# Sums of the adaLN columns turned in 32 by 32 blocks on VectorE, with the order of all instructions set anew, in a two-layer attention trunk

## The chip, the cores and the metric

The kernel runs on one core of a Trainium2 chip. The metric is the device time of one execution in microseconds. Engines are named as in the profile: PE (TensorE's matmuls) and PEld (its weight loads), DVE (VectorE), ACT (ScalarE), POOL (GpSimd), SP (SyncE, which issues nearly all transfers).

## What is computed

The input x has 256 rows of 1,024 in fp32, and c is one row of 1,024. Two layers follow each other; cut to what matters here:

```
c_act = silu(c)
for layer in range(2):
    ada = c_act @ w_ada[layer] + b_ada[layer]          # 1024 -> 3072
    shift, scale, gate = split(ada, 3)
    h = rms_norm(x, norm_g[layer]) * (1 + scale) + shift
    y = even_mixer(h, ...) if layer == 0 else odd_mixer(h, ...)
    x = x + gate * y
return rms_norm(x, final_g)
```

The even mixer is one input projection (2,840 columns), two groups of attention heads (a sliding window with sinks; a sparse one with a compressed, a selected and a window branch), a gate, and an output projection. The odd mixer projects to 4,096 columns, attends in blocks, gates and projects back.

## The kernel before, in words

**Layout.** Activations lie with features on the 128 partitions. `hhi` and `hlo` hold the normed input of a layer in two parts, `ghi` and `glo` the gated attention's output; each weight is split the same way, on ACT (`whi`, a cast) and on DVE (`wlo`, the rest), and every product is three matmuls, hi by hi, hi by lo and lo by hi (`mm3`). The weights come in through a ring of five buffers, `raw` (`raw_106` to `raw_110` in the rows below); `whi` and `wlo` have four buffers each. PSUM's banks are shared out as ps_pj (3), ps_s (2), ps_pt, ps_o and ps_m.

**The order.** No engine's code is in the order in which the work is written down. Each call is recorded as an operation with what it depends on (`Plan.record`, lines 242 to 277), and at the end `Plan.issue` emits all of them in the order of a table of some 3,000 numbers, `ORDER` (line 35 on), which thereby sets the order on each engine and on each queue. A second table, `FLIP`, lists the copies, scalings and affine steps that go to the other of ACT and DVE. In the profile all operations have the line of the recorded call, L276, so they are told apart by their tiles. `record` also keeps ACT's functions of different tables apart: an operation of one kind depends on all those of the other kind before it (line 273).

**The columns of shift and scale, layer 0.** `cz` holds silu(c) in column 0 of 32 columns for each of the 8 row blocks, zeros elsewhere, and a one at [:, KT, 0]. The features are done in groups of n = 1, 2, 2, 2 and 1 blocks of 128 (`START`, line 24). For a group `start_ada` (line 719 on) loads the columns of `w_ada` into whatever room is free (the tiles `qT`, `gate`, `oT`, `kTb`, `t`), and `start_sums` (line 731) forms the sums over the rows: the first d row blocks on DVE into `acc`, the others on PE, as fp32 matmuls with `cz` as weights in four tiles of 32 columns of the array side by side. So the sums of 128 columns come out along a row in one of four partitions (0, 32, 64 and 96) of the bank `ps_m`, with zeros in the other partitions. With n = 2 each of the four holds one block of shift or scale, all row blocks summed; with n = 1 two of them share a block, even row blocks in one and odd ones in the other. The rows are turned to columns: copied to `asb` (128x128, on ACT or DVE), turned by PE with `ident` (n = 2) or multiplied with the two columns of `blk` (n = 1), back into `ps_m`; DVE adds the biases from there into `shs`. Then `start_prep` makes `hhi` and `hlo` of these features by an affine step, and `start_mm` adds their products to the eight accumulators of the first projection.

**Layer 1's columns.** While layer 0 runs, DVE sums the rows of `w_ada[1]` into the fifth buffer of the ring (`raw_110`) by `ada_sums`, 16 passes of 1,024 columns, as loads come in between those for the weights. `ada_shift_scale` (line 476) then takes this sum over the partitions by four matmuls of 512 columns with `cz`, ACT copies them to a `t` tile, PE turns it in four pieces with `ident`, and DVE adds the biases from `ps_m` into `shs`. At the hand-over from layer 0 to layer 1 (lines 1132 to 1150) the row tile t is scaled by the reciprocal root of its mean square (each half on DVE or ACT), turned on PE, and `hhi` and `hlo` are made by affine steps with `shs`; the first product of layer 1 takes `hhi` as its right side.

Of the kernel before, what the change touches and what calls it, by code (L numbers as in the profile page):

```python
# [287 lines left out]
def tile_trunk(  # L288
# [187 lines left out]
    def ada_shift_scale(l, accs):  # L476
# [3 lines left out]
        for q in range(4):  # L480
            ids.append(T.matmul(pa[32 * q : 32 * q + 32, :], cz[:, KT, :], accs[q], start=True, stop=True, tile_position=(0, 32 * q)))
# [919 lines left out]
```

## Time and profile before

| what | value |
|---|---|
| median of 3 runs | 294.73 us (293.92 to 294.83) |
| the profiled execution's own time | 295.43 us |
| its span (first to last instruction) | 293.7 us |
| granted clock of TensorE | 0.996 |
| busy share: PE, PEld, DVE, ACT, POOL | 97%, 83%, 86%, 69%, 2% |
| read from memory | 70.32 MB |

The profile has one execution's instructions with start, duration, tile, shape and the operation whose end released a wait ("idle before, releaser"). The time lies 1.7 us over the span. A matmul of fp32 operands shows as two records, so a count of x16 is eight matmuls. The chain of work that ended last follows what released each instruction back from the end of the span.

### The profile page before, as it was taken

How to read it: one execution, taken by the hardware profiler on the slowest of the kernel's cores; microseconds unless marked ns; L12 is line 12 of the kernel's file. 1: busy time of each engine (PE TensorE's matmuls, PEld its weight loads, DVE VectorE, ACT ScalarE, POOL GpSimd, SP SyncE). 2: the span in 40 equal slices, each digit the busy share in tenths (PEclk: the TensorE clock that was granted, in tenths of full speed). 3: DMA queues.
4: the chain of work that ended last, by engine and by line, in shares of the span. 5: the costliest groups of instructions: out<-in, count | busy, mean ns of one | idle time of the engine just before them, and what ended most of it. 6: DMA issues, size and time to landing. Idle time of an engine off the chain costs nothing.

```text
span 293.7 us, 6077 instructions
## 1 busy us (share of the span) xinstructions
PE 283.5 (97%) x2244; PEld 243.5 (83%) x2244; DVE 253.0 (86%) x612; ACT 201.2 (69%) x513; POOL 5.5 (2%) x27
## 2 busy tenths in 40 slices
PE   8989999999999999999899999999999999999991
PEld 7868888997789888777667799999799899887891
DVE  0669999999999999999899868898699889889973
ACT  5554746695999999996398744466667377783821
POOL 2100000000000000000000000000000000000000
PEclk9999999999999999999999999999999999999998
DMA  7999999987996787799996449608927661604003
GB/s 260 364 385 377 383 355 353 311 287 237 342 400 212 264 281 293 213 323 361 305 372 216 146 143 329 243 4 296 351 71 249 237 234 34 227 27 145 1 15 129
DMA packets 50557, 71.76 MB, mean 244 GB/s; under 512 B 2792, under 2 KB 36192, under 8 KB 50528
## 3 DMA queue, kind: packets, MB, share of 16 engines
q1 hardware_dynamic: 50128, 70.95, 70.7%
q10 hardware_dynamic: 400, 0.43, 0.4%
q8 instruction: 17, 0.28, 0.4%
q14 instruction: 12, 0.10, 0.1%
HBM read 70.32 MB, written 1.06 MB: 243 GB/s over the span
## 4 chain that ended last, share of the span: by engine, by line
PE 73%; DVE 13%; DMA 8%; issue 2%; ACT 2%; SPq 0%; DVEq 0%
PE ps_pj L276 49%; PE ps_s L276 9%; PE ps_pt L276 6%; DVE raw L276 5%; PE ps_o L276 4%; PE ps_m L276 4%; DMA kTb<-in_w_ada_dram 3%; DMA raw<-in_w_ada_dram 2%; DVE wlo L276 2%; DMA qT<-in_w_ada_dram 2%; DMA xs<-in_x_dram 1%; DVE t L276 1%; DVE oT L276 1%; ACT t L276 1%; DVE bigA L276 1%
## 5 line engine op out<-in xcount | busy, mean ns | idle before, releaser
L276 ACT CAST whi<-raw 128x512 fp32r<-128x512 f32 (+2 forms) x108 | 71.6, 689 | 33.6 <-PE ps_pj L276 15.8
L276 DVE TENSOR_TENSOR wlo<-raw,whi 128x512 fp32r<-128x512 f32 (+2 forms) x92 | 70.8, 792 | 6.4 <-ACT whi L276 6.4
L276 PE MATMUL ps_pj<-hlo,whi 128*128 128x256 f32 x256 | 70.8, 284 | 0.0
L276 PE MATMUL ps_pj<-hhi,wlo 128*128 128x256 f32 x256 | 70.0, 284 | 0.3 <-DVE wlo L276 0.3
L276 PE MATMUL ps_pj<-hhi,whi 128*128 128x256 f32 x256 | 69.9, 284 | 0.0
L276 PEld LDWEIGHTS ps_pj<-hlo,whi 128*128 128x128 f32 x256 | 48.0, 189 | 0.6 <-issue 0.3
L276 PEld LDWEIGHTS ps_pj<-hhi,wlo 128*128 128x128 f32 x256 | 47.4, 189 | 0.7 <-DVE wlo L276 0.5
L276 PEld LDWEIGHTS ps_pj<-hhi,whi 128*128 128x128 f32 x256 | 47.4, 188 | 0.3
L276 ACT ACTIVATE sm<-sm,mn 128x256 f32<-128x256 f32 (+1 forms) x58 | 25.9, 449 | 6.9 <-DVE mn L276 6.9
L276 PE MATMUL ps_pj<-whi,hhi 128*128 128x512 f32 (+2 forms) x72 | 25.8, 368 | 0.5 <-ACT hhi L276 0.4
L276 PE MATMUL ps_pj<-whi,hlo 128*128 128x512 f32 (+2 forms) x72 | 26.1, 374 | 0.0
L276 PE MATMUL ps_pj<-wlo,hhi 128*128 128x512 f32 (+2 forms) x72 | 26.0, 370 | 0.0
L276 DVE SCALAR_TENSOR_TENSOR wlo<-raw,whi 128x512 fp32r<-128x512 f32 x32 | 20.6, 686 | 3.7 <-ACT whi L276 3.6
L276 PE MATMUL ps_pj<-wlo,ghi 128*128 128x512 f32 (+1 forms) x56 | 20.4, 368 | 0.0
L276 PE MATMUL ps_pj<-whi,ghi 128*128 128x512 f32 (+1 forms) x56 | 20.4, 369 | 0.0
L276 PE MATMUL ps_pj<-whi,glo 128*128 128x512 f32 (+1 forms) x56 | 20.0, 367 | 0.0
L276 ACT ACTIVATE sm<-sm,rc 128x256 f32<-128x256 f32 (+1 forms) x41 | 17.3, 449 | 2.3 <-DVE rc L276 2.3
L276 DVE SCALAR_TENSOR_TENSOR raw<-raw,cz,raw 128x1024 f32<-128x1024 f32 x14 | 17.9, 1276 | 1.0 <-DMA raw<-in_w_ada_dram 0.9
L276 DVE SCALAR_TENSOR_TENSOR acc<-raw,cz,acc 128x1024 f32<-128x1024 f32 x14 | 17.9, 1278 | 0.1
L276 PEld LDWEIGHTS ps_pj<-whi,hhi 128*128 128x128 f32 x72 | 13.6, 188 | 2.7 <-ACT hhi L276 1.2
L276 PEld LDWEIGHTS ps_pj<-whi,hlo 128*128 128x128 f32 x72 | 13.5, 188 | 2.5 <-DVE hlo L276 0.8
L276 PE MATMUL ps_pt<-ident,sm 128*128 128x128 f32 x87 | 15.5, 279 | 0.0
(252 smaller groups left out, 599.7 us busy)
## 6 DMA issues: line engine op xcount, KB each, us to landing
raw<-in_w_in_odd_dram SPq DMA_DIRECT2D x16, 1024.0 KB, 7.5
raw<-in_w_ada_dram SPq DMA_DIRECT2D x8, 1024.0 KB, 6.2
raw<-in_w_ada_dram SPq DMA_DIRECT2D x16, 512.0 KB, 5.2
raw<-in_w_in_even_dram SPq DMA_DIRECT2D x8, 652.0 KB, 7.2
raw<-in_w_in_even_dram SPq DMA_DIRECT2D x5, 1024.0 KB, 7.7
raw<-in_w_out_even_dram SPq DMA_DIRECT2D x4, 1024.0 KB, 5.4
raw<-in_w_out_odd_dram SPq DMA_DIRECT2D x4, 1024.0 KB, 5.0
qT<-in_w_ada_dram SPq DMA_DIRECT2D x12, 256.0 KB, 6.2
```

What stands on the lines that cost most here:

```text
L276: self.ops.append(dict(key=eng.key, deps=deps, fn=lambda: getattr(real, name)(*args, **kw)))
```

## The change

**The turning.** Instead of a copy, a turn on PE and adds from PSUM, DVE turns the sums straight from PSUM into SBUF in blocks of 32 by 32 (`V.transpose`, STREAM_TRANSPOSE in the rows), and the adds read SBUF. For that the four tiles of 32 array columns no longer hold a block each: tile q now takes columns 32q to 32q + 31 of every 128-column block (the strided `cq` and `aq`), so that a turn by 32 by 32 blocks puts each sum on its own partition. A group of n blocks turns 64n columns, layer 1's turns 512. With n = 1 each tile now sums all row blocks, in 64 columns instead of 128: the first group's sums are 32 matmuls of 64 columns (64 records) in place of 16 of 128, the last group's 20 (40 records) in place of 10.

**The tables.** An operation of a table kind now also depends on the first one of its own kind (`self.since[:1]`), so that the small activation that brings a table's load goes ahead of the others. `ORDER` and `FLIP` are new throughout.

```diff
-            deps |= set(self.before)
+            deps |= set(self.before + self.since[:1])
...
-            ids.append(T.matmul(pa[32 * q : 32 * q + 32, :], cz[:, KT, :], accs[q], start=True, stop=True, tile_position=(0, 32 * q)))
+            aq = accs.rearrange("p (b e) -> p b e", e=P)[:, :, 32 * q : 32 * q + 32]
+            ids.append(T.matmul(pa[32 * q : 32 * q + 32, :], cz[:, KT, :], aq, start=True, stop=True, tile_position=(0, 32 * q)))
         plan.group(ids)
         asb = t4()[:, :512]
-        copy(A, asb, pa)
-        pc = bank("m")
-        for o in range(0, 512, P):
-            T.transpose(pc[:, o : o + P], asb[:, o : o + P], ident)
-        pv = pc.rearrange("p (c h s e) -> p h s c e", c=4, h=2, s=2)[:, :, :, :, 0]
+        V.transpose(asb, pa)
+        pv = asb.rearrange("p (h s c e) -> p h s c e", h=2, s=2, e=32)[:, :, :, :, 0]
...
-            s_, j, ks = (q // 2, 0, range(q % 2, KT, 2)) if n == 1 else (q // 2, q % 2, range(KT))
-            cs = slice(j * P, (j + 1) * P)
-            tq = [(cz[:, k, :], w[k][:, s_, cs]) for k in ks if k >= d]
-            if d and 0 in ks:
-                tq.append((cz[:, KT, :], av[:, s_, cs]))
-            terms.append(tq)
+            cq = lambda v: v.rearrange("p s (j e) -> p (s j) e", e=P)[:, :, 32 * q : 32 * q + 32]
+            terms.append([(cz[:, k, :], cq(w[k])) for k in range(d, KT)] + ([(cz[:, KT, :], cq(av))] if d else []))
...
-        asb = sb([P, 2 * P], "asb", 2)
-        copy(A, asb[:, :P], pa[:, :P])
-        pc = bank("m")
+        asb = sb([P, 2 * P], "asb", 2)[:, : 64 * n]
+        V.transpose(asb, pa[:, : 64 * n])
...
-        if n == 1:
-            T.matmul(pc[:, 0:2], asb[:, :P], blk[:, 6:8], start=True, stop=True)
...
-            T.transpose(pc[:, :P], asb[:, :P], ident)
...
+        pv = asb.rearrange("p (s j e) -> p s j e", s=2, e=32)[:, :, :, 0]
+        V.tensor_tensor(shs[:, 0, :, gs], pv, bs, ALU.add)
+        V.tensor_tensor(shs[:, 0, 1, gs], shs[:, 0, 1, gs], ngT[:, gs], ALU.mult)
```

In all PE has 1,902 instructions in place of 1,885, DVE 619 in place of 615, ACT 430 in place of 434. Three transpositions of `asb`, four of `t`, two products with `blk`, and six copies of sums (two on DVE, four on ACT) go; six turns on DVE come. Of the copies and scalings that `FLIP` moves, three 128x384 copies (`kTb`) and two 128x512 ones (`bigA`) go from DVE to ACT, and three 128x128 scalings (`sm`) the other way, among others. In the start SP issues, behind x, both pieces of `qT0`, then the 384 columns of the first projection rows, a piece of `qT1`, and only then the 1,304 columns that stood second; the two pieces of `kTb` stood together behind `gate`, and now the first goes out between `gate`'s two pieces and the second still behind all of that group.

PE, in the start, around the second group's sums (`kTb` and `acc` with `cz`, into `ps_m_68`), among the products of the first projection. Before:

```order
L276 MATMUL ps_pj_101<-wlo_116,hhi 128x512
L276 MATMUL ps_pj_100<-wlo_116,hhi 128x512
L276 MATMUL ps_s_97<-wlo_116,hhi 128x512
L276 MATMUL ps_m_68<-kTb,cz 32x128 x8
L276 MATMUL ps_m_68<-acc_111,cz 32x128 x4
L276 MATMUL ps_s_98<-whi_112,hhi 128x512
L276 MATMUL ps_s_97<-whi_112,hlo 128x512
L276 MATMUL ps_m_68<-ident,asb_86 128x128
```

After:

```order
L275 MATMUL ps_s_98<-whi_112,hhi 128x512
L275 MATMUL ps_s_98<-wlo_116,hhi 128x512
L275 MATMUL ps_pt_90<-wlo_117,hhi 128x256
L275 MATMUL ps_m_68<-oT,cz 32x128 x8
L275 MATMUL ps_m_68<-kTb,cz 32x128 x8
L275 MATMUL ps_m_68<-acc_111,cz 32x128 x4
L275 MATMUL ps_s_97<-wlo_116,hhi 128x512
L275 MATMUL ps_o_70<-wlo_117,hhi 128x408
```

The group's first sums, `oT` with `cz`, which stood 17 rows ahead of `kTb`'s before, now stand next to them, and the transposition with `ident` four rows further on is gone.

PE, the last group's sums of the start (the same tiles, n = 1). Before:

```order
L276 MATMUL ps_o_70<-whi_113,hhi 128x408
L276 MATMUL ps_m_68<-kTb,cz 32x128 x8
L276 MATMUL ps_m_68<-acc_111,cz 32x128 x2
L276 MATMUL ps_pj_100<-whi_114,hlo 128x512
L276 MATMUL ps_pj_100<-whi_112,hhi 128x512
L276 MATMUL ps_m_68<-blk,asb_85 128x2
```

After:

```order
L275 MATMUL ps_pt_90<-wlo_119,hhi 128x256
L275 MATMUL ps_m_68<-kTb,cz 32x64 x16
L275 MATMUL ps_m_68<-acc_111,cz 32x64 x4
L275 MATMUL ps_pj_100<-whi_112,hhi 128x512
L275 MATMUL ps_pj_99<-whi_115,hlo 128x408
```

Ten matmuls of 128 columns became 20 of 64, and the product with `blk` went.

DVE, the end of layer 0, from the sum that frees `raw_109` to the last piece of layer 1's sums, which is loaded into the same buffer (`oT` and `glo` are the gated outputs, `sm` and `rc` the softmax's). Before:

```order
L276 SCALAR_TENSOR_TENSOR raw_110<-raw_109,cz,raw_110 128x1024
L276 TENSOR_SCALAR sm_126<-sm_126,rc_143 128x256
L276 TENSOR_SCALAR sm_126<-sm_126,rc_143 128x128
L276 SCALAR_TENSOR_TENSOR oT<-ps_o_70,oT 128x256
L276 TENSOR_TENSOR wlo_119<-raw_107,whi_115 128x1024
L276 SCALAR_TENSOR_TENSOR raw_110<-raw_106,cz,raw_110 128x1024 x2
L276 SCALAR_TENSOR_TENSOR oT<-ps_o_70,oT 128x256
L276 TENSOR_TENSOR wlo_116<-raw_108,whi_112 128x1024
L276 TENSOR_TENSOR glo<-oT,ghi 128x512
L276 SCALAR_TENSOR_TENSOR raw_110<-raw_109,cz,raw_110 128x1024 x2
```

After:

```order
L275 SCALAR_TENSOR_TENSOR raw_110<-raw_109,cz,raw_110 128x1024
L275 TENSOR_TENSOR wlo_118<-raw_107,whi_114 128x1024
L275 SCALAR_TENSOR_TENSOR oT<-ps_o_70,oT 128x256
L275 SCALAR_TENSOR_TENSOR raw_110<-raw_106,cz,raw_110 128x1024
L275 TENSOR_TENSOR wlo_119<-raw_107,whi_115 128x1024
L275 SCALAR_TENSOR_TENSOR raw_110<-raw_106,cz,raw_110 128x1024
L275 SCALAR_TENSOR_TENSOR oT<-ps_o_70,oT 128x256
L275 TENSOR_TENSOR wlo_116<-raw_108,whi_112 128x1024
L275 TENSOR_TENSOR glo<-oT,ghi 128x512
L275 SCALAR_TENSOR_TENSOR raw_110<-raw_109,cz,raw_110 128x1024 x2
```

The two products with `rc_143` are out of this stretch, and `wlo_118` is in it.

DVE, the hand-over, from the reciprocal root of the first row tile (`parts`) to the product of the second one's last piece with the gate (`t_96`); `rT` holds the biases and `raw_106`, `raw_107` layer 1's first weights. Before:

```order
L276 RECIPROCAL parts<-parts 128x1
L276 TENSOR_SCALAR rT<-rT 128x8
L276 TENSOR_SCALAR t_94<-xs,parts 128x512
L276 TENSOR_TENSOR shs<-ps_m_68,rT 128x2x4 x2
L276 TENSOR_TENSOR shs<-shs,rT 128x8
L276 TENSOR_TENSOR wlo_118<-raw_106,whi_114 128x512
L276 TENSOR_TENSOR wlo_116<-raw_107,whi_112 128x512
L276 TENSOR_TENSOR t_96<-ps_s_98,gate 128x512
```

After:

```order
L275 RECIPROCAL parts<-parts 128x1
L275 STREAM_TRANSPOSE t_93<-ps_m_68 128x512
L275 TENSOR_TENSOR wlo_119<-raw_106,whi_115 128x512
L275 TENSOR_TENSOR shs<-t_93,rT 128x2x4 x2
L275 TENSOR_TENSOR shs<-shs,rT 128x8
L275 TENSOR_TENSOR wlo_119<-raw_106,whi_115 128x512
L275 TENSOR_TENSOR wlo_116<-raw_107,whi_112 128x512
L275 TENSOR_TENSOR t_96<-ps_s_98,gate 128x512
```

The scaling of `xs` by `parts` left DVE (ACT has both halves now), the turn of `ps_m_68` came in, and one `wlo` stands ahead of `shs`.

More of the change, by code (lines that the diff above doesn't have):

```diff
@@ L511, in shift_scale_jobs @@
         r = [lambda u=u, h=h: ada_sums(l, [(512 * h, 512 * h + 512), (D + 512 * h, D + 512 * h + 512)], 2 * u, 2, raws[4][:, D * h : D * h + D]) for h in range(2) for u in range(4)]
-        return r + [lambda: ada_shift_scale(l, acs)]
+        return r + [lambda: ada_shift_scale(l, raws[4])]
     dp = ctx.enter_context(tc.tile_pool(name="dp", bufs=1, space=bass.MemoryType.DRAM))
@@ L753, in start_sums @@
                     ids.append(T.matmul(
-                        pa[32 * q : 32 * q + 32, :P],
+                        pa[32 * q : 32 * q + 32, : 64 * n],
                         tq[m][0],
@@ L762, in start_sums @@
             plan.group(ids[o : o + 8])
-        asb = sb([P, 2 * P], "asb", 2)
-        copy(A, asb[:, :P], pa[:, :P])
-        pc = bank("m")
+        asb = sb([P, 2 * P], "asb", 2)[:, : 64 * n]
+        V.transpose(asb, pa[:, : 64 * n])
         gs = slice(g, g + n)
         bs = bT[:, 0:16].rearrange("p (s j) -> p s j", s=2)[:, :, gs]
-        if n == 1:
-            T.matmul(pc[:, 0:2], asb[:, :P], blk[:, 6:8], start=True, stop=True)
-            V.scalar_tensor_tensor(shs[:, 0, 1, gs], pc[:, 1:2], bs[:, 1, :], ngT[:, gs], op0=ALU.add, op1=ALU.mult)
-            V.tensor_tensor(shs[:, 0, 0, gs], pc[:, 0:1], bs[:, 0, :], ALU.add)
-        else:
-            T.transpose(pc[:, :P], asb[:, :P], ident)
-            pv = pc[:, :P].rearrange("p (s j e) -> p s j e", s=2, e=32)[:, :, :, 0]
-            V.tensor_tensor(shs[:, 0, :, gs], pv, bs, ALU.add)
-            V.tensor_tensor(shs[:, 0, 1, gs], shs[:, 0, 1, gs], ngT[:, gs], ALU.mult)
+        pv = asb.rearrange("p (s j e) -> p s j e", s=2, e=32)[:, :, :, 0]
+        V.tensor_tensor(shs[:, 0, :, gs], pv, bs, ALU.add)
+        V.tensor_tensor(shs[:, 0, 1, gs], shs[:, 0, 1, gs], ngT[:, gs], ALU.mult)
     def start_row(g):
@@ L1084, in tile_trunk @@
     raws = ring["raw"][0]
-    acs = [raws[4][:, 512 * q : 512 * q + 512] for q in range(4)]
     ring["raw"] = [raws[:4], 0]
```

259 rows, old and new, of tables (FLIP, ORDER) are left out of this document.

## The prediction

> **What bounds the kernel now.** I read the per-core line first, then the busy time by stretches, then the chain of work that ended last, then the timeline around its waits. The one core is granted its full clock, so no term below is a change of clock:
>
> ```profile
> core 0: 293.7 us, clock 0.996
> ```
>
> The stretches (length, busy time of each engine with instruction counts, clock, share of the DMA engines, GB/s):
>
> ```profile
> core 0: us, PE busy (x) PEld busy (x) DVE busy (x) ACT busy (x) POOL busy (x), PEclk, DMA share, GB/s
> 20.00:60.00 40.00, 40.00 (x273) 34.54 (x273) 37.58 (x82) 25.18 (x62) 0.00 (x0) 1.00 1.03 352
> 60.00:103.00 43.00, 43.00 (x415) 36.47 (x415) 42.39 (x149) 38.71 (x124) 0.38 (x3) 1.00 0.85 291
> 103.00:146.00 43.00, 42.63 (x306) 33.01 (x302) 41.94 (x87) 36.28 (x96) 0.32 (x1) 1.00 0.86 296
> ```
>
> PE is without a gap from 20 to 103 us, and DVE is nearly so: it idles 2.42 us in 20 to 60, 0.61 in 60 to 103, 1.06 in 103 to 146. The transfers are full until 60 us. So layer 0 is bound by PE with DVE a hair behind, and there is hardly room for either to take on work. The chain (start, length, what) shows where the end is set by something else:
>
> ```profile
> 11.01 7.55 DMA kTb<-in_w_ada_dram
> ...
> 134.45 6.87 DMA raw<-in_w_ada_dram
> 141.42 1.29 DVE raw L276
> ...
> 145.22 1.14 DVE wlo L276
> ...
> 152.34 0.82 ACT t L276 x2
> ```
>
> Three places, then: a transfer at 11 to 18.6 us, DVE (held once by a transfer) until 146, and the hand-over to layer 1 at 151 to 153.6. After that the chain is PE almost to the end, and the change leaves that stretch and the tail as they were. The first and the last two places are where a moved order can act; 20 to 103 us is where removed PE work counts.
>
> **The change part by part.** *A, the start.* PE's one long stop and the work behind it:
>
> ```profile
> 18.61 0.64 PE L276 MATMUL ps_m<-kTb,cz 128*32 128x128 f32 x16 [1.12 <-DMA kTb<-in_w_ada_dram]
> 20.05 0.62 ACT L276 CAST whi<-raw 128x512 fp32r<-128x512 f32 x1 [2.64 <-DMA raw<-in_w_in_even_dram]
> ```
>
> PE waits 1.12 us for the last piece of kTb, and 1.4 us later ACT waits for the next rows of the projection weights. The new queue order puts the same bytes ahead of both, so both should land when they did, and PE can't come out of the start earlier than those landings let it. What goes is the copy and the transposition between kTb's sums and the next factors (20.0 us), of which one short DVE instruction is left: I take -0.2. If kTb lands sooner, as one of its two pieces now goes out earlier, up to half of the stop goes (-0.6); if the rows that were moved back come late, +0.5.
>
> *B, the PE work that goes from the PE-bound stretch.*
>
> ```profile
> 19.98 0.28 PE L276 MATMUL ps_m<-ident,asb 128*128 128x128 f32 x1
> 48.61 0.28 PE L276 MATMUL ps_m<-blk,asb 128*128 128x2 f32 x2
> 150.74 0.60 PE L276 MATMUL ps_m<-ident,t 128*128 128x128 f32 x4
> ```
>
> Four transpositions take 0.60 and one 0.28, so each further one costs PE (0.60 - 0.28) / 3 = 0.11 us, the rest being the pipeline's depth. Two of them lie after 20 us (the third is in A), and the pair with blk at 48.6 costs something between 0.11 and 0.28, say 0.18: 2 x 0.11 + 0.18 = 0.4. With PE unbroken from 20 to 103 us this comes off the chain: -0.4 (bounds -0.2, if DVE holds PE at once, and -0.5).
>
> *C, the sums of the single blocks in 64 columns.* The last group is issued as 40 records of 64 columns where 20 of 128 stood (each fp32 product shows as two records); the first as 64 where 32 stood, but that one is ahead of PE's 1.12 us stop and costs nothing as long as the stop is there. Prices:
>
> ```profile
> 11.09 0.81 PEld L276 LDWEIGHTS ps_m<-qT,cz 128*32 128x32 f32 x32
> 11.10 1.08 PE L276 MATMUL ps_m<-qT,cz 128*32 128x128 f32 x32
> 47.26 0.66 PE L276 MATMUL ps_m<-kTb,cz 128*32 128x128 f32 x16
> ```
>
> A further record costs (1.08 - 0.66) / 16 = 0.026 us, and the weight load of a record 0.81 / 32 = 0.025. If the columns set the pace, 40 records of 64 cost what 20 of 128 did: 0. If the loads do, which are no shorter for fewer columns, 20 more records cost 20 x 0.025 = +0.5. The two prices are so alike that I believe the loads, and take +0.4. The Trainium skill speaks against the change here: "TensorE: Matmul & The Clock Gate", the section "Wait — 56ns, not 53.3ns?", says that matmuls never start less than about 25 ns apart, however few columns they have; by that this term would be +0.5 (an estimate from the page), and the trace's 0.026 us for 128 columns in four tiles side by side already lies at that floor. No run here shows 64 columns.
>
> *D, DVE's wait for the last piece of layer 1's sums.* The piece's buffer is released by the sum that starts at 132.69 (ends 133.97); SyncE issues the load at 133.99, and DVE needs it at 140.47, but gets it 0.95 us later:
>
> ```profile
> 132.69 1.28 DVE L276 SCALAR_TENSOR_TENSOR raw<-raw,cz,raw 128x1024 f32<-128x1024 f32 x1
> 133.88 0.54 DVE L276 TENSOR_SCALAR sm<-sm,rc 128x256 f32<-128x256 f32 x2
> 133.99 0.88 SPq L276 DMA_DIRECT2D raw<-in_w_ada_dram  x2
> 134.34 0.42 DVE L276 SCALAR_TENSOR_TENSOR oT<-ps_o,oT 128x256 f32<-128x256 f32 x1
> 134.68 1.22 DVE L276 TENSOR_TENSOR wlo<-raw,whi 128x1024 fp32r<-128x1024 f32 x1
> 135.81 2.60 DVE L276 SCALAR_TENSOR_TENSOR raw<-raw,cz,raw 128x1024 f32<-128x1024 f32 x2
> 138.32 0.42 DVE L276 SCALAR_TENSOR_TENSOR oT<-ps_o,oT 128x256 f32<-128x256 f32 x1
> ...
> 139.79 0.68 DVE L276 TENSOR_TENSOR glo<-oT,ghi 128x512 fp32r<-128x512 f32 x1
> 141.42 2.60 DVE L276 SCALAR_TENSOR_TENSOR raw<-raw,cz,raw 128x1024 f32<-128x1024 f32 x2 [0.95 <-DMA raw<-in_w_ada_dram]
> ```
>
> Between release and need stood 0.54 + 2 x 0.42 + 2 x 1.22 + 2.60 + 0.68 = 7.10 us by duration, passed in 6.50 (instructions overlap a little). The new order takes the two sm products (0.54) out of this stretch and puts a third wlo (1.22) in: 7.78, which at the same ratio passes in 7.12. If the load lands as long after its issue as now (7.4 us), 0.3 of the 0.95 us is left: -0.7. Bounds: -0.95, and 0. The 0 comes from DVE itself: up to here it has more work than before. Three turns of 128 columns at the copy's price and two of 64 at some 0.2, less the two copies that go, are 3 x 0.29 + 0.4 - 0.58 = 0.7; one more scaled row (0.42), one more 512-column copy and one 512-column scaling less, 0.68 - 0.49 (rows below):
>
> ```profile
> 13.85 0.68 DVE L276 COPY bigA<-ps_pj 128x512 f32<-128x512 f32 x1
> 19.54 0.29 DVE L276 COPY asb<-ps_m 128x128 f32<-128x128 f32 x1 [1.92 <-PE ps_m L276]
> 151.11 0.49 DVE L276 TENSOR_SCALAR t<-xs,parts 128x512 f32<-128x512 f32 x1
> ```
>
> Together +1.3 us, all of it before 60 us, where DVE's 2.42 us of idle time is the cover. If that cover doesn't lie where the work does, DVE comes to this place as late as the load, and the wait goes without a gain.
>
> *E, the hand-over to layer 1.* Behind layer 0's last adds DVE takes the reciprocal of the row's root; from there:
>
> ```profile
> 150.53 1.12 ACT L276 CAST whi<-raw 128x512 fp32r<-128x512 f32 x2
> 150.91 0.16 DVE L276 RECIPROCAL parts<-parts 128x1 f32<-128x1 f32 x1
> 151.51 0.23 DVE L276 TENSOR_TENSOR shs<-ps_m,rT 128x8 f32<-128x8 f32 x2
> 151.56 0.72 ACT L276 ACTIVATE t<-xs,parts 128x512 f32<-128x512 f32 x1
> 151.77 0.17 DVE L276 TENSOR_TENSOR shs<-shs,rT 128x8 f32<-128x8 f32 x1
> 151.86 1.29 DVE L276 TENSOR_TENSOR wlo<-raw,whi 128x512 fp32r<-128x512 f32 x2
> 153.64 0.50 PE L276 MATMUL ps_pj<-whi,hhi 128*128 128x512 f32 x1 [0.42 <-ACT hhi L276]
> ```
>
> Now the reciprocal ends at 151.07, DVE and ACT scale one half each, and ACT's first affine part starts at 152.34, 1.27 us later. After the change ACT scales both halves (2 x 0.72) and casts one weight part (1.12 / 2 = 0.56) ahead of it, 1.9 us with their overlap; DVE turns 512 columns (0.68, as a copy of that size from PSUM), makes one wlo (0.65) and the shifts (0.40), 1.73 us. ACT is the later: 1.9 - 1.27 = +0.6. PE isn't: five more 512-column products stand ahead of layer 1's first one than before, but the four transpositions are gone and PE waits 0.42 for hhi now. Bounds: 0, if the chain reaches the reciprocal with ACT already through its casts and the halves overlap, and +1.1, if DVE's turn costs what its 1,024-column passes do (1.22): 1.22 + 0.65 + 0.40 = 2.27, 1.0 more than now, and some 0.1 for the wait of PE behind it.
>
> Sum: -0.2 - 0.4 + 0.4 - 0.7 + 0.6 = -0.3 us. The profiled execution took 295.43 us, 0.70 over the median of 294.73: 295.1 for it, and 294.4 for the median.
>
> **The rivals.** *The order closes the gaps.* Each term ends at its good side: A -0.6, B -0.4, C 0, D -0.95, E 0, in sum -1.95, 292.8 us. For it speaks that all of these waits are small against the work around them, so that a few moved instructions fill them; against it, that ACT's work ahead of layer 1 grew by half a row.
>
> *DVE eats its own gain.* Of the 1.3 us of added work about 0.95 isn't covered by idle time in the start, so DVE comes to the last piece as late as the load does, the wait is gone and nothing is won by it; D is 0: -0.2 - 0.4 + 0.4 + 0 + 0.6 = +0.4, 295.1 us. Against it speak the 2.42 us of idle time before 60.
>
> *DVE becomes the bound, slower.* The turns cost more than copies. If 512 columns take 1.22 us and those of 128 in proportion more than 0.29, little of the start's idle time is left, DVE's 1.3 us reach the stretch from 103 us on, which is DVE's, and only the 0.95 us of wait there takes some back: +0.35; with E at +1.1 the sum is -0.2 - 0.4 + 0.4 + 0.35 + 1.1 = +1.25, 296.0 us. It decides from the point at which a 512-column turn takes over 0.85 us, where DVE's path in E gets as long as ACT's 1.9. No row of before shows a turn. The Trainium skill has one for bf16: "VectorE: DVE Perf Modes", section "The three transpose paths", gives 311 ns for 128x128, in blocks of 32 by 32; if it grew with the columns, 512 would take an estimated 1.24 us, which is this rival.
>
> **How the numbers follow.** The forecast's own range, with its terms' bounds set against each other, is -1.0 to +0.7 us, 293.7 to 295.4. Some 0.3% (0.88 us) is what a measurement of this kernel tells from no change. Chances: forecast 0.38 (0.08 faster, 0.28 the same, 0.02 slower); closed gaps 0.27, all faster; DVE eats its gain 0.13 (0.11 the same, 0.02 slower); DVE as the bound 0.22 (0.04 the same, 0.18 slower). That is 0.35 faster, 0.43 the same, 0.22 slower. Cases of both signs hold much of the chance, so the range reaches from just under the closed gaps, 292.6, to the slower rival, 296.0.
>
> **What would show it.** Right: PE's stop for kTb still 0.6 to 1.2 us near 17 us; 40 records of the last kTb group in about 1.1 us; the last piece of the sums waited for by under 0.4 us; a 512-column turn at 0.6 to 0.8 us; 1.8 to 2.0 us from the reciprocal to the first affine part, ended by ACT. Wrong: a turn over 0.85 us or turns of 128 columns well over 0.29; DVE idle in 20 to 60 us gone; PE gaps in 20 to 103 us, where none were; the 64-column records at half the time; or a new wait for a transfer of layer 1's weights behind 146 us, since those loads too were moved.

## The result, and the profile after

The changed kernel takes 292.83 us (median of 5 runs, 292.53 to 293.58), the kernel before 294.27 in the same comparison (293.67 to 294.83): a ratio of 0.995, with a 95% interval of 0.993 to 0.997, or 1.4 us less. In a later comparison the unchanged pair gave 293.08 and 294.41, a ratio of 0.9948 (0.9929 to 0.9967). The profiled execution took 293.58 us, with this span and clock:

```profile
core 0: 291.6 us, clock 0.993
```

The stretches of after, to set beside those of before:

```profile
20.00:60.00 40.00, 40.00 (x293) 34.75 (x291) 38.76 (x88) 25.05 (x60) 0.00 (x0) 1.00 1.08 375
60.00:103.00 43.00, 43.00 (x411) 37.35 (x409) 42.24 (x152) 39.08 (x124) 0.36 (x2) 1.00 0.77 268
103.00:146.00 43.00, 42.85 (x306) 32.44 (x305) 42.29 (x85) 36.36 (x95) 0.00 (x0) 1.00 0.88 305
```

VectorE idles 1.24 us in 20 to 60 us where it idled 2.42: the turns and the rest of its new work went into idle time, and PE has no gap there.

What PE waits for in all (total, times, longest), first in the profile of before, then in that of after, less a wait of 1.1 us for `ones` at the start that every run has:

```profile
PE ps_m L276 <- DMA kTb<-in_w_ada_dram: 1.1, 1, 1.1
...
PE ps_s L276 <- DVE wlo L276: 0.8, 1, 0.8
PE ps_pj L276 <- ACT hhi L276: 0.4, 1, 0.4
PE ps_pj L276 <- DVE wlo L276: 0.3, 1, 0.3
```

```profile
...
PE ps_m L275 <- DMA oT<-in_w_ada_dram: 0.6, 1, 0.6
PE ps_pj L275 <- ACT hhi L275: 0.4, 1, 0.4
PE ps_m L275 <- DVE acc L275: 0.2, 1, 0.2
PE ps_pj L275 <- DVE glo L275: 0.2, 1, 0.2
```

The wait for kTb became a shorter one for another tile of the same group, the waits for wlo at 146 and 166 us are gone, and the 0.4 for hhi is another one: it stands at 14 us, not at the hand-over. VectorE around the last piece of layer 1's sums, and the hand-over, in the timeline of after:

```profile
130.76 1.28 DVE L275 SCALAR_TENSOR_TENSOR raw<-raw,cz,raw 128x1024 f32<-128x1024 f32 x1
...
137.94 1.23 DVE L275 TENSOR_TENSOR wlo<-raw,whi 128x1024 fp32r<-128x1024 f32 x1 [0.55 <-ACT whi L275]
...
139.69 2.60 DVE L275 SCALAR_TENSOR_TENSOR raw<-raw,cz,raw 128x1024 f32<-128x1024 f32 x2
```

```profile
149.37 0.16 DVE L275 RECIPROCAL parts<-parts 128x1 f32<-128x1 f32 x1
149.44 0.70 DVE L275 STREAM_TRANSPOSE t<-ps_m 128x512 f32<-128x512 f32 x1
149.56 1.34 ACT L275 ACTIVATE t<-xs,parts 128x512 f32<-128x512 f32 x2 [0.48 <-DVE parts L275]
150.81 0.61 ACT L275 CAST whi<-raw 128x512 fp32r<-128x512 f32 x1
151.32 0.80 ACT L275 ACTIVATE t<-ps_pj,shs 128x128 f32<-128x128 f32 x2
152.60 0.50 PE L275 MATMUL ps_pj<-whi,hhi 128*128 128x512 f32 x1
```

The buffer is freed at 132.04 in place of 133.97, the last piece is there when VectorE comes (no wait in its row), and VectorE waits 0.55 for ScalarE's cast instead. From the reciprocal to the first affine part it is 1.95 us where it was 1.43 (150.91 to 152.34), and layer 1's first product starts at 152.60 instead of 153.64. That is 1.04 of the 2.1 us between the spans; the other half comes behind this point.

### The profile page after: what moved, and what is told of

Same layout as the page of the kernel before. It is cut to its first block, busy times and chain, and to the rows that moved or that the text cites. A ratio compares the mean times of both kernels' runs of the same rounds, so it can differ in the third digit from the quotient of the medians.

```text
span 291.6 us, 6173 instructions
## 1 busy us (share of the span) xinstructions
PE 282.9 (97%) x2285; PEld 242.9 (83%) x2285; DVE 252.0 (86%) x616; ACT 200.5 (69%) x509; POOL 5.2 (2%) x27
## 4 chain that ended last, share of the span: by engine, by line
PE 66%; DVE 21%; DMA 7%; issue 3%; ACT 1%; SPq 1%; DVEq 0%
PE ps_pj L275 46%; PE ps_s L275 8%; PE ps_pt L275 5%; DVE wlo L275 4%; PE ps_o L275 4%; DVE raw L275 3%; DVE acc L275 3%; DMA qT<-in_w_ada_dram 3%; PE ps_m L275 3%; DVE t L275 2%; DMA raw<-in_w_out_even_dram 2%; DMA raw<-in_w_in_even_dram 2%; DVE sm L275 2%; DVE oT L275 1%; DVE bigA L275 1%
## 5 line engine op out<-in xcount | busy, mean ns | idle before, releaser
L275 ACT ACTIVATE sm<-sm,mn 128x128 f32<-128x128 f32 (+1 forms) x58 | 26.0, 451 | 14.2 <-DVE mn L275 14.2
L275 PE MATMUL ps_pt<-ident,sm 128*128 128x128 f32 x87 | 16.1, 279 | 0.0
L275 DVE TENSOR_TENSOR t<-ps_pj,tb 128x512 f32<-128x512 f32 (+2 forms) x22 | 12.1, 587 | 4.5 <-PE ps_pj L275 4.4
```

Source lines behind the costliest of these rows:

```text
L275: self.ops.append(dict(key=eng.key, deps=deps, fn=lambda: getattr(real, name)(*args, **kw)))
```

## The experiments

**A second profile of before (before_again).** Unchanged code.

> The kernel before, unchanged, for a second profile: the first one was 1.1 us over the median of its runs, and it is open which of its waits (1.12 us for kTb, 0.95 for the last piece, 0.78 for wlo, 0.42 for hhi) are there in every execution. Theory 1 expects those from 141 us on to be there again.

It ran 294.44 us, its span is 292.7. PE's waits here, less the one for `ones`, then VectorE's last piece and the first product:

```profile
...
PE ps_pj L276 <- ACT hhi L276: 0.4, 1, 0.4
PE ps_s L276 <- ACT hhi L276: 0.3, 1, 0.3
PE ps_pj L276 <- DVE t L276: 0.3, 1, 0.3
PE ps_pj L276 <- DVE wlo L276: 0.3, 1, 0.3
```

```profile
139.93 2.60 DVE L276 SCALAR_TENSOR_TENSOR raw<-raw,cz,raw 128x1024 f32<-128x1024 f32 x2
...
150.10 0.15 DVE L276 RECIPROCAL parts<-parts 128x1 f32<-128x1 f32 x1
...
152.83 0.50 PE L276 MATMUL ps_pj<-whi,hhi 128*128 128x512 f32 x1 [0.41 <-ACT hhi L276]
```

Neither the wait for kTb, nor the 0.95 us for the last piece, nor the 0.78 for wlo is there. What recurs is 0.41 for hhi at the hand-over and 0.3 for wlo at 165 us. So Theory 1's waits from 141 us on were only in part there again: the two transfer waits on which the prediction built are not in every execution (the one for kTb is 0.55 us in b_turn's profile and under 0.2 in those of b_acc and b_nowait; for the last piece see b_nowait below).

**The turning alone, in the old order (b_turn).** Each copy became a turn in the same place, the TensorE turns went:

```diff
-        copy(A, asb[:, :P], pa[:, :P])
...
+        V.transpose(asb, pa[:, : 64 * n])
...
-            T.transpose(pc[:, :P], asb[:, :P], ident)
```

> The kernel before in its old order of instructions, with the new turning alone: all six turns on VectorE stand where the copies stood, the single blocks' sums are in 64 columns, and the copies and the nine turning products are gone from ScalarE and TensorE. Theory 1 (the gain is in the order: waits at 141, 146, 153 and 166 us that went): little is gained, TensorE's 0.4 us less work against a 0.7 us turn in VectorE's chain ahead of the hand-over, 293.9 to 294.9 us, and the wait of 0.95 us for the last piece of the sums is still there. Theory 2 (the gain is in the turning): most of the 1.4 us, 292.6 to 293.4 us.

294.70 us against 294.34, ratio 1.001 (0.9998 to 1.0021): no gain. The single blocks' sums are in 64 columns here too, but two row blocks of one tile follow each other where in after the four tiles take turns, and the last group's 40 records took 1.04 us (46.81 to 47.85), against 0.76 in after. Its turn for layer 1 lies ahead of the sum of squares:

```profile
148.46 0.71 DVE L280 STREAM_TRANSPOSE t<-ps_m 128x512 f32<-128x512 f32 x1
...
153.05 0.50 PE L280 MATMUL ps_pj<-whi,hhi 128*128 128x512 f32 x1 [0.41 <-ACT hhi L280]
```

**The old turning, in the new order (a_old).** Copy, TensorE turn and adds from PSUM in all six places. At the start's places:

```diff
-        V.transpose(asb, pa[:, : 64 * n])
...
+            A.copy(asb[:, :P], pa[:, :P])
...
-        pv = asb.rearrange("p (s j e) -> p s j e", s=2, e=32)[:, :, :, 0]
...
+            T.transpose(pc[:, :P], asb[:, :P], ident)
...
+            pv = pc[:, :P].rearrange("p (s j e) -> p s j e", s=2, e=32)[:, :, :, 0]
```

> The kernel after in its new order, with the old turning: copy, TensorE turn or product with two columns, and adds from PSUM, each placed right where the VectorE turn stood, the TensorE part two or three products later; 128 columns for the single blocks. Theory 1 (order): keeps most of the gain, 0.3 to 0.8 us slower than after for the TensorE work that returns, 293.1 to 293.6 us. Theory 2 (turning): loses it, 294.0 to 294.6 us.

298.16 us, ratio 1.013 (1.0112 to 1.0148): slower than before by some 3.8 us, and beyond both ranges. Busy time in 20 to 60 us, and the second group's turn:

```profile
20.00:60.00 40.00, 37.34 (x243) 30.49 (x243) 34.26 (x75) 20.98 (x48) 0.00 (x0) 1.00 1.04 358
```

```profile
18.78 0.40 PE L279 MATMUL ps_m<-acc,cz 128*32 128x128 f32 x8
...
21.18 0.27 PE L279 MATMUL ps_m<-ident,asb 128*128 128x128 f32 x1
22.53 0.50 PE L279 MATMUL ps_s<-whi,hhi 128*128 128x512 f32 x1 [1.08 <-ACT hhi L279]
```

The edit did not do what the expectation said: on TensorE ten products, not two or three, came to stand between the sums and the turn, so the factors came at 21.5 us (20.1 in after) and TensorE waited for hhi. It shows that the new order leaves the start's factors no 1.4 us to spare; it doesn't show what a well-placed old turn would cost there.

**The old turning for layer 1 alone (a_old1).** Copy ahead of the root on ScalarE, four turns on TensorE where before had them, the start untouched:

```diff
-        V.transpose(asb, pa)
...
+        A.copy(asb, pa)
+        pc = bank("m")
...
+        for o in range(0, 512, P):
+            T.transpose(pc[:, o : o + P], asb[:, o : o + P], ident)
```

> The kernel after with the old turning for layer 1 alone (copy on ScalarE ahead of the root, four turns on TensorE eight products later, as in the kernel before); the start keeps the new turning. Theory 3 (the 5.3 us that the old turning cost in the new order come from the start, where TensorE waits for hhi four times): within 0.6 us of after, as the hand-over gains 0.7 us on VectorE and pays 0.4 on TensorE and 0.5 on ScalarE. Rival (the old turning costs as much at the hand-over): 1.5 us or more over after.

293.13 us against 293.08 for after on the same chip (after_again): the kind of turning at the hand-over makes no difference. Theory 3 holds in so far as a_old's loss came from the start.

> The kernel after, unchanged, as the measure for its variants on the same chip: 292.4 to 293.3 us.

It took 293.08 us, inside that range.

**One VectorE instruction moved in before (b_wlo).** In rows of VectorE's order:

```diff
-TENSOR_TENSOR wlo_118<-raw_107,whi_114 128x1024
 SCALAR_TENSOR_TENSOR raw_110<-raw_109,cz,raw_110 128x1024
 RECIPROCAL rc_143<-den_140 128x4
 TENSOR_TENSOR rc_143<-rc_143,gt 128x4
 SCALAR_TENSOR_TENSOR raw_110<-raw_109,cz,raw_110 128x1024
+TENSOR_TENSOR wlo_118<-raw_107,whi_114 128x1024
```

> The kernel before with one VectorE instruction moved: the wlo of 1.22 us that stands ahead of the two passes which free the buffer of the last piece is put behind them (its two products on TensorE follow three places later). The load can go out about 1.1 us earlier. Theory 1: VectorE's wait of 0.95 us near 141 us falls under 0.2, and as VectorE's chain leads from there to layer 1, the time falls by 0.5 to 0.9, to 293.4 to 293.8 us. Rival: the next transfer (layer 1's first weights) or TensorE's own queue takes over, and the time stays within 0.2 us of 294.3.

298.52 us, ratio 1.0161 (1.0139 to 1.0182): much slower, against both. The load went out at 133.39 us, hardly sooner than in before (133.99) and before_again (133.53), as VectorE now stood 1.31 us for ScalarE's softmax sums ahead of the second pass. TensorE stood for the wlo that came late, and its granted clock (the column after POOL) was halved afterwards:

```profile
134.55 0.50 PE L280 MATMUL ps_s<-wlo,ghi 128*128 128x512 f32 x1 [2.76 <-DVE wlo L280]
```

```profile
130.00:134.50 4.50, 1.79 (x14) 1.05 (x10) 3.16 (x6) 3.85 (x13) 0.00 (x0) 1.00 0.99 366
...
136.00:139.20 3.20, 3.20 (x11) 2.42 (x10) 2.90 (x3) 0.48 (x1) 0.00 (x0) 0.50 1.01 383
139.20:142.00 2.80, 2.80 (x27) 1.91 (x25) 0.00 (x0) 1.52 (x2) 0.00 (x0) 1.00 0.68 181
```

**The reverse move in after (a_wlo).** The same wlo put back ahead of the two passes, in rows of VectorE's order; with it, one scaling of `bigA` on ScalarE went behind a copy, and its three transpositions on TensorE went some places later:

```diff
+TENSOR_TENSOR wlo_118<-raw_107,whi_114 128x1024
 SCALAR_TENSOR_TENSOR raw_110<-raw_109,cz,raw_110 128x1024
 RECIPROCAL rc_143<-den_140 128x4
 TENSOR_TENSOR rc_143<-rc_143,gt 128x4
 SCALAR_TENSOR_TENSOR raw_110<-raw_109,cz,raw_110 128x1024
-TENSOR_TENSOR wlo_118<-raw_107,whi_114 128x1024
```

> The kernel after with the reverse of the move tried on the kernel before: the wlo of 1.22 us put back ahead of the passes that free the last piece's buffer. The load goes out about 1.2 us later, at 133.2, and lands near 140.6. Theory 1 (this release is where the new order gains): VectorE waits 0.6 to 0.9 us for the last piece again and the time rises by 0.4 to 0.9 over after. Rival (TensorE is the bound from 140 us to the hand-over, and VectorE has that time to spare): under 0.2 us.

295.73 us against 293.08, 2.65 us more, and not for the reason expected: the wlo, moved forward, waited for ScalarE's cast, everything behind it came late, and TensorE stood for softmax tiles, one of them the `bigA` that had been moved too, with a clock of 0.55 after it:

```profile
130.77 1.23 DVE L279 TENSOR_TENSOR wlo<-raw,whi 128x1024 fp32r<-128x1024 f32 x1 [1.76 <-ACT whi L279]
```

```profile
134.03 0.84 PE L279 MATMUL ps_pt<-ident,bigA 128*128 128x128 f32 x3 [0.88 <-ACT bigA L279]
```

```profile
136.00:139.00 3.00, 3.00 (x12) 1.84 (x12) 2.62 (x3) 1.80 (x3) 0.00 (x0) 0.55 0.92 317
```

Both moves fail as tests of the buffer's release, since each brought a wait of its own; how much of a_wlo's loss is the wlo's and how much the moved `bigA`'s is open.

**The wait for the last piece by itself (b_nowait).** The load left out of before:

```diff
+            if (l, k0, cuts[0][0]) == (1, 6, 512):
+                plan.n += 1
+            else:
                 Y.dma_start(w[:, :, o : o + e - b], src[:, k0 : k0 + kk, b:e])
```

> The kernel before without the load of the last piece of layer 1's sums: its two passes read what stands in the buffer already, so layer 1's shift and scale are not the reference's. VectorE waits no more at 141 us, and 1 MB of transfer is gone. Theory 1 (that wait leads to layer 1): 0.6 to 0.95 us less, 293.4 to 293.8 us. Rival (the wait is covered, as TensorE or the next loads set the hand-over): within 0.2 us of before.

293.75 us against 294.41, ratio 0.9983 (0.997 to 0.9995): 0.2 to 0.9 us less, at the lower end of Theory 1's range. Layer 1's first product came at 151.94. By the medians (0.66 us) the load's wait and its bandwidth together are worth about half of the whole gain, by the interval a tenth to two thirds; the wait itself was 0.95 us in the first profile of before, 0.35 in that of b_acc, and none in those of before_again and b_turn.

**Two more loads on the hand-over (a_dup, a_half).** The 512-column turn done twice, or the first half of the scaling moved back to VectorE by leaving it out of the list of steps that change engines:

```diff
+        V.transpose(asb[:, 512:], pa)
         V.transpose(asb, pa)
```

```diff
-1220 1311 1312 1317 1337 1338 1343 1388 1389 1394 1414 1415 1420 1608 1614 1615 1618 1619 1637 1643 1646 1658
+1220 1311 1312 1317 1337 1338 1343 1388 1389 1394 1414 1415 1420 1614 1615 1618 1619 1637 1643 1646 1658
```

> The kernel after with the 512-column turn done twice (the second result is not used), 0.70 us more on VectorE between the reciprocal and layer 1's shifts. If ScalarE and TensorE set the hand-over as in the prediction (VectorE has about 0.2 us of slack there): +0.3 to +0.6 us, 293.1 to 293.4 us. If TensorE alone is the bound in the hand-over and VectorE has room: under +0.2. If VectorE's chain is the bound: +0.7, 293.5 us or more.

> The kernel after with the first half of the hand-over's scaling back on VectorE (behind the turn), as in the kernel before. ScalarE's way from the reciprocal to the first affine part falls from 1.9 to 1.3 us, VectorE's rises from 1.75 to 2.24. If the later of the two sets the hand-over, as in the prediction's term E: +0.2 to +0.4 us over after. If TensorE is the bound there: within 0.15.

a_dup took 293.55 us, ratio 0.998 to before (0.9969 to 0.9991), where after's ratios are 0.995: slower than after by some 0.5 to 0.9 us, between the first case and the third, but no run of after stood beside it. a_half took 293.05 against 293.08, as its rival had it. Reciprocal and first affine part, of a_dup and of a_half:

```profile
148.87 0.15 DVE L279 RECIPROCAL parts<-parts 128x1 f32<-128x1 f32 x1
...
151.26 0.80 ACT L279 ACTIVATE t<-ps_pj,shs 128x128 f32<-128x128 f32 x2 [0.35 <-DVE shs L279]
```

```profile
149.35 0.16 DVE L279 RECIPROCAL parts<-parts 128x1 f32<-128x1 f32 x1
...
151.54 0.81 ACT L279 ACTIVATE t<-ps_pj,shs 128x128 f32<-128x128 f32 x2 [0.57 <-DVE shs L279]
```

2.39 and 2.19 us in place of 1.95: with more on VectorE, shs comes last and ScalarE waits for it, by the sizes that the later of the two paths gives. The traces show the effect; in the times a_half's 0.24 us is too small to be told.

**One wait behind the hand-over (b_acc).** In before, the gate's first pass put behind the wlo that TensorE waits for at 166 us:

```diff
-TENSOR_SCALAR acc_111<-raw_106,cz 128x1024
...
+TENSOR_SCALAR acc_111<-raw_106,cz 128x1024
```

> The kernel before with one VectorE instruction moved: the first pass of the gate's sums (0.74 us) goes behind the first wlo of the stretch, which TensorE waits for at 166.05 us. Theory 4 (a part of the gain is waits behind the hand-over, which the prediction took as left alone): that wait of 0.3 to 0.45 us goes, and the time falls by as much, to 293.9 to 294.1 us. Rival (the wait moves to the next wlo or to the gate's sums): within 0.15 us of before.

294.61 us against 294.41, ratio 1.0009 (0.9993 to 1.0024): nothing, as the rival had it. The wait was in the first profile of before

```profile
165.37 0.28 PE L276 MATMUL ps_pj<-hhi,whi 128*128 128x256 f32 x1
165.48 0.28 PE L276 MATMUL ps_pj<-hlo,whi 128*128 128x256 f32 x1
166.05 0.39 PE L276 MATMUL ps_pj<-hhi,wlo 128*128 128x256 f32 x1 [0.29 <-DVE wlo L276]
```

and in b_acc's list of PE's waits it stands under another name, at 169.85 us:

```profile
PE ps_pj L280 <- DVE bigA L280: 0.4, 1, 0.4
```

**Columns or records (a_32).** The single blocks' sums in halves of 32 columns, the second half (`32:64`, the scales' columns) behind the first:

```diff
-                        pa[32 * q : 32 * q + 32, : 64 * n],
-                        tq[m][1],
+                        pa[32 * q : 32 * q + 32, z],
+                        tq[m][1][:, 0, :] if n == 1 else tq[m][1],
...
+                        pa[32 * q : 32 * q + 32, 32:64],
+                        tq[m][1][:, 1, :],
```

> The kernel after with the single blocks' sums in 32 columns instead of 64, twice as many: 80 records for the last group, at 46 to 47.5 us, which took 0.70 us as 40 records. If a record has a least price of 0.025 us whatever its columns: 2.0 us. If four tiles side by side share it and only columns count: about 0.7 to 0.8 us.

The last group's sums in the timelines of before (behind its row of kTb), after and a_32, first and last rows:

```profile
47.73 0.39 PE L276 MATMUL ps_m<-acc,cz 128*32 128x128 f32 x4
```

```profile
46.30 0.65 PE L275 MATMUL ps_m<-kTb,cz 128*32 128x64 f32 x32
46.77 0.29 PE L275 MATMUL ps_m<-acc,cz 128*32 128x64 f32 x8
```

```profile
46.36 0.46 PE L279 MATMUL ps_m<-kTb,cz 128*32 128x32 f32 x32
...
47.01 0.25 PE L279 MATMUL ps_m<-acc,cz 128*32 128x32 f32 x6
```

20 records of 128 columns took 47.26 to 48.12, 0.86 us; 40 of 64 columns 46.30 to 47.06, 0.76; 80 of 32 columns 46.36 to 47.26, 0.90. Forty more records cost 0.14 us, so with the four tiles in turn columns count and records hardly. b_turn's 1.04 us for the same 40 records of 64 columns in another sequence shows that this holds for that sequence only. The ends of matmuls are modelled, but from the first record to the start of the next product it is 0.78, 0.70, 0.82 and, in b_turn, 0.97 us, the same picture.

**The profiles side by side.** Reciprocal, first affine part, layer 1's first product, span, and what is left from that product to the end:

| kernel | reciprocal | affine | first product | span | left |
|---|---|---|---|---|---|
| before | 150.91 | 152.34 | 153.64 | 293.7 | 140.1 |
| before_again | 150.10 | 151.53 | 152.83 | 292.7 | 139.9 |
| b_turn | 150.33 | 151.76 | 153.05 | 293.0 | 139.9 |
| b_acc | 150.41 | 151.84 | 153.13 | 293.0 | 139.9 |
| b_nowait | 149.21 | 150.64 | 151.94 | 291.8 | 139.9 |
| after | 149.37 | 151.32 | 152.60 | 291.6 | 139.0 |
| after_again | 149.16 | 151.10 | 152.39 | 291.3 | 138.9 |
| a_old1 | 149.04 | 150.99 | 152.28 | 291.5 | 139.2 |
| a_half | 149.35 | 151.54 | 152.84 | 291.9 | 139.1 |
| a_32 | 148.72 | 150.66 | 151.96 | 290.9 | 138.9 |

The last column parts the kernels by their order alone: 139.9 to 140.1 us in the old one, with the old turning or the new, 138.9 to 139.2 in the new one, with the new turning or, for layer 1, the old. The four kernels left out fall in with these: b_wlo 139.9; a_dup and a_wlo 139.1, a_old, with the old turning everywhere, 139.2. TensorE's records behind that product are the same in both orders, 1,049, but for one transposition more in the old. So 0.7 to 1.2 us of the gain lie behind the hand-over and belong to the order. Up to the first product the four complete kernels of the old order (all but b_nowait) come at 153.16 on the mean, and after, after_again, a_old1 and a_32 at 152.31: another 0.85 us. This half is less sure than the last column, as the two executions of before alone differ by 0.81 us at this point, and the two halves together come to more than the 1.4 us of the medians.

Where it arises can be read from these eight profiles. Not in the start: the last of the 240 products of the first projection starts at 64.71 to 65.18 us in the old order and at 64.61 to 65.24 in the new one. But layer 1's first weights are loaded into the buffer that VectorE's second pass over `raw_106` frees, and SyncE issues this load at 137.97 to 138.44 us in the old order, at 136.94 to 137.25 in the new one. ScalarE waits for it, and in before_again, b_acc and after_again VectorE then waits for ScalarE's cast. In before_again:

```profile
145.98 0.62 ACT L276 CAST whi<-raw 128x512 fp32r<-128x512 f32 x1 [2.53 <-DMA raw<-in_w_in_odd_dram]
...
146.63 0.69 DVE L276 TENSOR_TENSOR wlo<-raw,whi 128x512 fp32r<-128x512 f32 x1 [0.57 <-ACT whi L276]
```

In after_again:

```profile
145.04 0.62 ACT L275 CAST whi<-raw 128x512 fp32r<-128x512 f32 x1 [2.53 <-DMA raw<-in_w_in_odd_dram]
```

From the start of this cast to the reciprocal it is 4.11 to 4.12 us in before_again, b_acc, after and after_again; in the other four it is longer (4.5 to 5.2), so there the weights were not what came last. In b_nowait, with 1 MB less to load, the cast did not wait for them, and the reciprocal came at 149.21. No run moved this load by itself.

## Why the prediction was right or wrong

The time lies inside the range, and the sign is the forecast's; but the gain is 1.4 us where the sum said 0.3, beyond the forecast's own range and between it and the rival of closed gaps. That the time is inside is owed to the width of the range, made to hold the rivals of both signs; of the sum's terms only E came out as worked, and half of the gain comes from a stretch that the sum left out.

**The first step that failed** is that the change leaves the stretch behind the hand-over as it was. It took 0.7 to 1.2 us from it. Nearly the same instructions stand there in both kernels, but in another order. Of the gain, 0.45 us is the wait for wlo at 166 us (0.57 from the start of the product ahead of it to its own, where that one follows its own predecessor by 0.11), which is in every profile of the old order but b_acc's, where one move turned it into another wait, and in none of the new order; one transposition of the row tile (0.11 us) stands ahead of the first product now; and 0.1 us lies behind TensorE's last matmul, from whose start to the end it is 6.54 us in the four complete profiles of the old order and 6.43 to 6.45 in the new one's. The rest, some 0.3 us, is spread over steps of under 0.15 us and not settled.

**A** rested on a stop of 1.12 us that is not in the second profile of before; after shows 0.61 for oT in one profile and nothing in the other. By the end of the first projection, at 65 us, no gain is to be seen beyond the 0.5 us by which executions differ.

**B** is not confirmed: b_turn takes the same TensorE work away and isn't faster. It also puts 0.71 us on VectorE ahead of the hand-over, so the two can't be told apart in its time; but they can in its trace, well ahead of there. Two products of the first projection start at 22.54 and 59.86 us in before_again and at 22.47 and 59.79 in b_turn, 37.32 us apart in both, with two transpositions and the products with blk between them in the one and not in the other. The third group's transposition does save 0.1 us where it stood, but TensorE comes to that group's sums 0.2 us later than to the products ahead of them, for reasons that are open, and the last group's sums take 0.19 us more, about as much as the products with blk had cost.

**C** was mis-sized: +0.4 was taken, and the 64-column sums take 0.76 us where the 128-column ones took 0.86, so about -0.1. The inference from the two equal prices, 0.026 and 0.025 us, to the loads as the bound was wrong for sums whose tiles take turns; a_32 settles it. In b_turn's sequence the price is about +0.2. The Trainium skill's rule that I set beside it ("TensorE: Matmul & The Clock Gate", "Wait — 56ns, not 53.3ns?", no less than about 25 ns from start to start) doesn't hold for four tiles side by side in these runs: 80 records of 32 columns in 0.90 us are 11 ns each, or 22 ns for each of the 40 products, the pipeline's depth included.

**D** had the right mechanism in the execution that was profiled: earlier release, no wait. As a price for the median it was taken from one execution, in which the wait was 0.95 us; taking it away whole, with its transfer, gave 0.2 to 0.9 us. The reciprocal comes 1.3 us earlier on the mean of the new order's profiles (149.1, over after, after_again, a_old1, a_half and a_32, against 150.4 over the four complete ones of the old order), more than this wait. The release does come earlier, but what hangs on it is at least as much the next load, layer 1's first weights, which the prediction named only as a possible new wait: in before_again, without the wait for the last piece, the reciprocal followed the landing of those weights. How the 1.3 us are shared out between the two isn't settled. The bound at 0, VectorE late by its added work, did not come: its idle time in 20 to 60 us fell by 1.2 us, which is that work.

**E** came out as worked: 1.95 - 1.43 = +0.5 us from the reciprocal to the first affine part where +0.6 was taken, ended by ScalarE, with the turn at 0.70 us where the copy's 0.68 was used, and VectorE's path growing past it by the sizes of a_half and a_dup. As a_old1 has the same 1.95 us, the loss belongs to ScalarE's added work and not to the turn. The five more products that the prediction saw ahead of layer 1's first one are not there: the same layer-0 products stand ahead of it in both orders, and only their places differ. The rival of VectorE as the bound falls with it: turns cost little more than copies.

The means of all turns of each size in after (count, busy time, mean ns):

```profile
L275 DVE STREAM_TRANSPOSE asb<-ps_m 128x128 f32<-128x128 f32 x3 | 0.9, 317 | 0.5 <-PE ps_m L275 0.5
L275 DVE STREAM_TRANSPOSE t<-ps_m 128x512 f32<-128x512 f32 x1 | 0.7, 699 | 0.0
...
L275 DVE STREAM_TRANSPOSE asb<-ps_m 128x64 f32<-128x64 f32 x2 | 0.5, 246 | 0.0
```

128 columns take 317 ns, which agrees with the Trainium skill's 311 ns for 128x128 in bf16 ("VectorE: DVE Perf Modes", "The three transpose paths"); but 512 take 699, not four times as much: by the three sizes about 1 ns per column comes on top of some 0.18 us.

Which of the two theories, then? The turning alone, in the old order, gains nothing. The new order with the old turning at the hand-over keeps all of the gain. That the new order would do with the old turning in the start as well was not shown, since a_old tested it badly. And "the new order" stands for three things that no run parts: the new `ORDER`, the new `FLIP` (of which a_half takes back one step) and the added dependence.

## What to carry to other kernels

Before a wait is priced, see whether it is in a second execution: of the waits of the first profile here, the two for transfers (1.12 and 0.95 us) and one for an instruction behind them (0.78) were gone in the second, while two for instructions (0.42 and 0.29) recurred to a tenth. Where a whole order is set anew, compare it in every stretch up to the end, by the time from a common instruction to the last one, also where the instructions are the same. Where one load no longer holds the work up, look at the next one in the queue. And in a queue as full as this, a single instruction moved by hand brings a new wait as easily as it removes one.

## What the runs showed of the hardware

A stop of TensorE of 2.76 us, or two of 0.88 and 0.61 us within 3 us, was followed by some 3 us at a granted clock of 0.50 to 0.55, in which a 512-column product took 0.43 us from start to start instead of 0.23. An estimate from these figures: 3.2 us at 0.50 and 3.0 us at 0.55 cost 1.6 and 1.35 us, about what b_wlo and a_wlo lost beyond the stops themselves (1.4 and 1.2 us). A stop of 1.08 us in a_old was not followed by it: the clock is 1.00 in its row for 20 to 60 us. The Trainium skill describes such a gate ("TensorE: Matmul & The Clock Gate", "Part 1: The HAM clock gate": half clock after an idle window of about 3.4 us); here less than that was enough.
